# Hybrid diffusion trunk on one core: stores of q, k, v from GpSimd and ScalarE, shared rope tables, residual loaded during the attention, differential softmax normalised on the output

## Chip, cores, metric

The kernel runs on one core of a Trainium2 chip. The metric is device time in microseconds (us), lower is better. Engines are called PE (TensorE), PEld (its weight loads), DVE (VectorE), ACT (ScalarE), POOL (GpSimd) and SP (SyncE); a "q" behind a name is that engine's instruction queue. L12 is line 12 of the kernel file. Layers are counted from 0.

## What is computed

One inference step of a two-layer trunk for 128 context tokens and 1024 latent tokens (a 16 x 64 grid), width 1024, all float32. In each layer:

```python
h = adaln(x, g_attn, m[0], m[1])                  # modulated RMS norm
q, k, v of A, B, C = split(h @ w_in)              # RMS norm on every q and k
q, k of B and C = rope(q, k)                      # latent tokens only
oa = neighborhood_attn(qa, ka, va, cache_na, rpb) # 4 heads of 64, window 8 x 16 with bias
ob = window_attn(qb, kb, vb, cache_sw, sink)      # 8 query heads, 2 key heads, |i-j| <= 128
oc = diff_attn(qc, kc, vc, cache_da, lam)         # 4 heads, all latent keys
x  = x + m[2] * (concat(oa, ob, oc) @ w_out)
x  = x + m[5] * conv_ffn(adaln(x, g_ffn, m[3], m[4]))
```

Each of the attentions also reads 256 cached keys and values; the context tokens attend to each other alone. The six modulation vectors m come from a matrix of 1024 x 6144 per layer. The differential attention is what the change rewrites:

```python
o1 = softmax(q1 @ k1.T) @ v
o2 = softmax(q2 @ k2.T) @ v
o  = rmsnorm(o1 - lam * o2, subln_g) * (1 - lam_init)
```

The outputs are x and, for the context tokens, the keys and values of both layers.

## The kernel before

Activations lie transposed: features on the 128 partitions, the 1156 columns (context, latent, a zero column at each border) along the free axis, cut into three chunks of about 386. A product of float32 matrices is three PE passes over a high and a low part of each operand (`gemm`, L496), so weights and activations are split on ACT and DVE or POOL before use (`wload`, L377 and L378; `norm_apply`, L483 and L484).

The order of the work is written out in `PLAN`: 18 column blocks of the input projection (`inproj`), with the four heads of the differential attention C (`attnC`) among them, "C:14+12" being two blocks interleaved and "c:0" a head. A block of q or k goes through, for each chunk: 24 matmuls, the norm's sum by a ones matrix (L523), the reciprocal root on ACT, DVE and POOL (L441 to L444), its product on POOL (L525), for B and C the rotation with a table loaded from memory (L531 to L536), the split into high and low (L559, L560), and a store to a scratch tensor in memory `d` (L542 to L565). v blocks are transposed on PE and stored likewise (L587), and the context part of k and v goes to the output `kvT` (L528, L580). Each head then reads its q, k and v back from `d` in the layout it needs: q and k by loads issued on POOL (L605 and L615; in C L695 and L699), v by loads on SP.

In `attnC` a pair of score rows (one for each component) of 128 queries and 1280 keys gets its exponentials (L682) and their sums, and then:

```python
735  nc.vector.reciprocal(ss, ss)
736  nc.vector.tensor_tensor(ss, ss, lam, op=ALU.mult)
737  nc.gpsimd.tensor_scalar(P2[0][:, :n], P2[0][:, :n], ss[:, 0:1], 0.0, op0=ALU.mult, op1=ALU.add)
738  nc.vector.scalar_tensor_tensor(P2[0][:, :n], P2[1][:, :n], ss[:, 1:2], P2[0][:, :n], op0=ALU.mult, op1=ALU.add)
```

so that the combined rows are normalised before they are transposed (L649) and multiplied with v (L658). `subln` follows for each pair of heads (L763 to L769), and the pair's output goes to the scratch `odr` (L757).

After the last block come the four heads of A (`attnA`), which normalise on the output instead (`rows_over`, L670: four transposes of the row sums; L905). Its bias tiles are loaded by SP into seven buffers (L855). The residual x (L296, 4.73 MB by the tile's shape) is loaded back behind A in the program's text, from the input in layer 0 and from the scratch `xsp` in layer 1; then B (`attnB`). The output projection has a part for C (i = 1) and one for A (i = 0), both from `odr` (`outproj_part`, L283), and one for B. In layer 0 eight pieces of the modulation matrix (`mod_piece`, four tiles `mraw` of 0.52 MB each, L388; two matmuls a tile, L392) stand four before each of the first two parts, with three buffers.

The program's text doesn't set the order of instructions on the engines: a scheduler with its own model of time fills each engine's queue. Every queue, SP's of transfers among them, then runs strictly in that order.

## Time and profile before

| | us |
|---|---|
| runs shown: median (lowest, highest) of 3 | 3601.14 (3599.38, 3604.77) |
| profiled execution, its own time | 3596.75 |
| its span, first to last instruction | 3595.0 |
| PE busy, share of the span | 3328.8 (93%) |
| DVE | 2146.0 (60%) |
| ACT | 1513.5 (42%) |
| POOL | 1054.7 (29%) |
| mean DMA rate over the span | 91 GB/s |

Busy shares are averages over stages with different limits; the stages, and what ends each wait, tell more. The granted clock (PEclk) is 1 at 2.4 GHz and 0.5 at 1.2 GHz; a mean between them says that a stretch saw both. A wait is put down to the instruction that released it last.

### The profile page before, as it was taken

To read this page: it belongs to the slowest core of one execution; us is meant where nothing else is said; L and a number is where in the kernel's file an instruction comes from. 1 tells how busy PE (TensorE), PEld (TensorE's weight loads), DVE (VectorE), ACT (ScalarE), POOL (GpSimd) and SP (SyncE) were. 2 spreads that over 40 slices of the span, in tenths; PEclk is the share of its full clock that TensorE was granted. 3 is DMA by queue.
4 is the path that set the end of the run, shared out by engine and by line. 5 is a ranking of instruction groups with operands and counts; after the bars stand their busy time and mean duration, and the time that the engine had idled before them with its cause. 6 is when DMAs were issued, how large, how long until landed. Compare 5 with 4: busy or idle time off the path is not lost. (4 is left out here: it accounts for less than half of the span.)

```text
span 3595.0 us, 54059 instructions
## 1 busy us (share of the span) xinstructions
PE 3328.8 (93%) x20334; PEld 3011.7 (84%) x20334; DVE 2146.0 (60%) x4646; ACT 1513.5 (42%) x2909; POOL 1054.7 (29%) x1170
## 2 busy tenths in 40 slices
PE   6799995999999999999997999868999999999999
PEld 4688773767889999999985877746878999999999
DVE  5567783445567755776575767944547544544455
ACT  4456664446432322222243566635674322232222
POOL 6545563011520111111155455532126111111110
PEclk9899997989999999999998999979999999999999
DMA  5543429532112212222134434385201111111112
GB/s 196 141 115 103 115 89 284 159 105 44 56 39 80 86 66 67 88 88 71 47 119 124 125 103 110 93 229 123 56 20 48 39 45 42 42 37 45 43 42 94
DMA packets 190675, 325.02 MB, mean 90 GB/s; under 512 B 58928, under 2 KB 132800, under 8 KB 190032
## 3 DMA queue, kind: packets, MB, share of 16 engines
q1 hardware_dynamic: 176752, 273.67, 24.8%
q0 software_dynamic: 13664, 47.91, 6.4%
q8 instruction: 161, 2.64, 0.3%
q14 instruction: 98, 0.80, 0.1%
HBM read 269.35 MB, written 56.36 MB: 91 GB/s over the span
## 5 line engine op out<-in xcount | busy, mean ns | idle before, releaser
L496 PE MATMUL mm<-h,whl 128*128 128x386 f32 (+2 forms) x4824 | 970.7, 351 | 27.2 <-DVE t L443 21.9
L496 PEld LDWEIGHTS mm<-h,whl 128*128 128x128 f32 x4824 | 881.5, 195 | 56.0 <-DVE t L443 30.9
L496 PE MATMUL s<-h,whl 128*128 128x386 f32 (+2 forms) x3960 | 740.3, 342 | 13.3 <-ACT h L483 6.7
L496 PEld LDWEIGHTS s<-h,whl 128*128 128x128 f32 x3960 | 704.4, 190 | 28.9 <-DVE h L484 13.5
L378 POOL TENSOR_TENSOR whl<-wraw,whl 128x1024 fp32r<-128x1024 f32 x88 | 211.4, 2402 | 1353.3 <-ACT whl L377 1267.2
L682 ACT ACTIVATE P<-P,nm 128x1280 f32<-128x1280 f32 (+4 forms) x360 | 345.5, 961 | 195.7 <-DVE nm L730 85.4
L377 ACT ACTIVATE whl<-wraw 128x1024 fp32r<-128x1024 f32 (+1 forms) x214 | 211.5, 990 | 469.1 <-PE s L496 275.4
L496 PE MATMUL s<-ah,whl 128*128 128x384 f32 (+1 forms) x1268 | 357.0, 342 | 1.6 <-DVE x L914 1.2
L651 ACT ACTIVATE pt<-tb 128x512 f32<-128x512 f32 (+2 forms) x456 | 237.0, 541 | 121.8 <-PE tb L649 119.1
L914 DVE SCALAR_TENSOR_TENSOR x<-mm,m,x 128x128 f32<-128x128 f32 (+3 forms) x357 | 176.1, 514 | 179.1 <-PE mm L496 178.5
L649 PE MATMUL tb<-ident,P 128*128 128x128 f32 x1600 | 264.7, 282 | 14.2 <-DVE P L738 9.5
L914 DVE SCALAR_TENSOR_TENSOR x<-s,m,x 128x128 f32<-128x128 f32 (+3 forms) x347 | 170.0, 513 | 169.9 <-PE s L496 169.5
L658 PE MATMUL pv<-pt,v 128*64 128x128 f32 x3200 | 260.3, 284 | 3.7 <-ACT pt L651 2.9
L649 PEld LDWEIGHTS tb<-ident,P 128*128 128x128 f32 x1600 | 181.8, 141 | 78.8 <-issue 44.4
L496 PE MATMUL mm<-ah,whl 128*128 128x384 f32 (+1 forms) x844 | 244.5, 340 | 1.4 <-DVE x L914 1.4
L496 PEld LDWEIGHTS s<-ah,whl 128*128 128x128 f32 x1268 | 233.8, 189 | 5.9 <-DVE x L914 1.7
L658 PEld LDWEIGHTS pv<-pt,v 128*64 128x64 f32 x3200 | 170.2, 136 | 77.2 <-issue 46.4
L679 PE MATMUL s<-k,q 128*128 128x256 f32 (+2 forms) x816 | 182.7, 339 | 39.9 <-DMA k<-d 28.1
L496 PE MATMUL s<-al,whl 128*128 128x384 f32 (+1 forms) x634 | 215.1, 339 | 0.0
L496 PE MATMUL mm<-o,whl 128*128 128x384 f32 (+1 forms) x792 | 171.8, 352 | 43.4 <-ACT o L636 41.3
L959 ACT ACTIVATE ah<-yv 128x384 fp32r<-128x384 f32 x132 | 69.4, 526 | 277.6 <-DVE yv L957 277.6
L496 PEld LDWEIGHTS mm<-o,whl 128*128 128x128 f32 x792 | 139.7, 192 | 53.6 <-ACT o L636 42.6
(199 smaller groups left out, 5018.7 us busy)
## 6 DMA issues: line engine op xcount, KB each, us to landing
wraw<-wup SPq DMA_DIRECT2D x88, 512.0 KB
mraw<-wmod SPq DMA_DIRECT2D x48, 512.0 KB
mraw<-wmv SPq DMA_DIRECT2D x96, 256.0 KB
wraw<-wdn SPq DMA_DIRECT2D x64, 384.0 KB
k<-d POOLq DMA_DIRECT2D x80, 288.5 KB, 6.0
wraw<-win SPq DMA_DIRECT2D x36, 512.0 KB
rope<-rope SPq DMA_DIRECT2D x36, 386.0 KB
d<-hl SPq DMA_DIRECT2D x28, 386.0 KB
```

The lines of the kernel that those rows point to most:

```text
L377: nc.scalar.activation(hl[:, 0, :n], raw[:, :n], AF.Copy)
L378: lo_eng.tensor_tensor(hl[:, 1, :n], raw[:, :n], hl[:, 0, :n].bitcast(F32), op=ALU.subtract)
L496: nc.tensor.matmul(ps, w_, r_[:, a:b], start=(i == 0), stop=(i == tot - 1))
L649: nc.tensor.transpose(t[:, 128 * j:128 * j + 128], it[0], self.ident)
L651: nc.scalar.activation(pt[:, :n], t[:, :n], AF.Copy)
L658: nc.tensor.matmul(ps[64 * i:64 * i + 64, :128], V[:, vb], pts[g // 4][:, 128 * (g % 4):128 * (g % 4) + 128], start=first[i], stop=left[i] ...
L679: nc.tensor.matmul(dst, q, view(ks[i]), start=(i == 0), stop=(i == 1))
L682: self.nc.scalar.activation(P[:, :n], P[:, :n], AF.Exp, scale=-1.0, bias=nm, accum_out=sums)
L914: nc.vector.scalar_tensor_tensor(xx, ps[:, s - a:e - a], m[:, col + ob, v:v + 1], xx, op0=ALU.mult, op1=ALU.add)
L959: nc.scalar.activation(ah[:, o:o + n], y, AF.Copy)
```

## The change

Seven edits stand together. Stores of q and k (and of the attention outputs of A and C to `odr`) are issued by POOL instead of SP, stores of v by ACT, and the store of k to the output moves behind the split. The rope table of a chunk is kept for the other block of an interleaved pair. The residual is loaded after the last bias load of A's second head, and with it the operands of the output projection for C. The modulation pieces are placed two before the part for C and six before that for A, with five buffers. In C the component rows are combined unnormalised, with the weight lam * sum1 / sum2 for the second, and the output is multiplied by 1 / sum1 for four query blocks at a time; `subln` follows at the second and the last of them.

```diff
-NM0, NMC = 8, 3
+NM0, NMC = 8, 5
@@ run
+                        self.rope = {}
                         gens = [self.inproj(ip, step[0], int(b)) for b in step[2:].split("+")]
...
                 x = xp.tile([128, KT, XW], F32, name="x")
-                for t in range(3):
-                    self.loadx(x, t)
                 ab, abs_ = self.open("oab")
+                with self.tc.issue_after(self.amark[1].ins):
+                    ow1 = self.loado(ab, 1)
+                    for t in range(3):
+                        self.loadx(x, t)
...
-                    for j in todo[4 - 4 * i:8 - 4 * i]:
+                    for j in todo[:2] if i else todo[2:]:
                         self.mod_piece(l, j, ab, self.mm(), NMC)
-                    self.outproj_part(x, ab, i)
+                    self.outproj_part(x, ow1 if i else self.loado(ab, 0), i)
@@ inproj, q and k
-                if not isq and ci == 0:
-                    nc.sync.dma_start(a["kvT"][l, KOUT[b]], qg[:, C0:C0 + SEQ])
                 if g != "A":
-                    cs = ip.tile([128, 2, 386], F32, name="rope", bufs=NR_I)[:, :, :n]
-                    nc.sync.dma_start(cs, a["rope"][0 if g == "B" else 1, :, :, c0:c1])
+                    if (g, ci) not in self.rope:
+                        cs = ip.tile([128, 2, 386], F32, name="rope", bufs=NR_I)[:, :, :n]
+                        nc.sync.dma_start(cs, a["rope"][0 if g == "B" else 1, :, :, c0:c1])
+                        self.rope[g, ci] = cs
+                    cs = self.rope[g, ci]
...
-                            nc.sync.dma_start(dst[:, i, :, c0:c1], hl[:, i, :n].bitcast(F32))
+                            nc.gpsimd.dma_start(dst[:, i, :, c0:c1], hl[:, i, :n].bitcast(F32))
                     else:
-                        nc.sync.dma_start(dst[:, :, c0:c1].rearrange("h p w -> p h w"), hl[:, :, :n].bitcast(F32))
+                        nc.gpsimd.dma_start(dst[:, :, c0:c1].rearrange("h p w -> p h w"), hl[:, :, :n].bitcast(F32))
+                if not isq and ci == 0:
+                    nc.gpsimd.dma_start(a["kvT"][l, KOUT[b]], qg[:, C0:C0 + SEQ])
@@ inproj, v (the store to kvT likewise)
-                nc.sync.dma_start(dst[ci].rearrange("t p c -> p t c"), vs)
+                nc.scalar.dma_start(dst[ci].rearrange("t p c -> p t c"), vs)
@@ attnC
+            sums = ap.tile([128, 8], F32, name="sums", bufs=2)
...
-                    nc.vector.reciprocal(ss, ss)
-                    nc.vector.tensor_tensor(ss, ss, lam, op=ALU.mult)
-                    nc.gpsimd.tensor_scalar(P2[0][:, :n], P2[0][:, :n], ss[:, 0:1], 0.0, op0=ALU.mult, op1=ALU.add)
+                    r = sums[:, q0 + i:q0 + i + 1] if q0 is not None else ss[:, 2:3]
+                    nc.vector.reciprocal(r, ss[:, 0:1])
+                    nc.vector.reciprocal(ss[:, 1:2], ss[:, 1:2])
+                    nc.vector.scalar_tensor_tensor(ss[:, 1:2], ss[:, 1:2], lam[:, 1:2], ss[:, 0:1], op0=ALU.mult, op1=ALU.mult)
                     nc.vector.scalar_tensor_tensor(P2[0][:, :n], P2[1][:, :n], ss[:, 1:2], P2[0][:, :n], op0=ALU.mult, op1=ALU.add)
...
+                if q0 in (2, 6):
+                    R = self.rows_over(sums[:, q0 - 2:q0 + 2], 1)[rows]
+                    oo = O[rows, L0 + 128 * (q0 - 2):L0 + 128 * (q0 + 2)]
+                    nc.vector.tensor_tensor(oo, oo, R, op=ALU.mult)
+                    if h % 2 == 1:
+                        for c0, c1 in NCHUNK[:1] if q0 == 2 else NCHUNK[1:]:
+                            self.subln(ap, O, c0, c1)
             if h % 2 == 1:
-                nc.sync.dma_start(self.odr[OT["C"] + h // 2], O)
+                nc.gpsimd.dma_start(self.odr[OT["C"] + h // 2], O)
@@ attnA
-                nc.sync.dma_start(bt, self.a["bias"][l, h, :, i])
+                self.lastb = nc.sync.dma_start(bt, self.a["bias"][l, h, :, i])
                 bias.append(bt)
+            self.amark[h] = self.lastb
```

The three loads of `oraw` that began `outproj_part` are now the function `loado`, otherwise unchanged. Because of the scheduler the rows of every engine move. Three places matter here.

The first is SP's queue in layer 0, where the last block of the in-projection (d_9) is stored and the loads for A begin (w_4 and d_4 are the v of A's first pair of heads, kc a cache tile). Before, and now:

```order
L531 DMA rope<-rope 128x2x386
L296 DMA x<-xT 128x8x386
L296 DMA x<-xT 128x8x384
L565 DMA d_9_4993<-hl 128x2x386
L296 DMA x<-xT 128x8x386
L374 DMA wraw<-woac 128x1024
L565 DMA d_9_4993<-hl 128x2x384
L757 DMA odr_544<-O 128x1156
L565 DMA d_9_4993<-hl 128x2x386
L618 DMA kc<-kc 128x256
L846 DMA v<-w_4_3744 128x16x64
L847 DMA v<-d_4_3510 128x64
```
```order
L537 DMA rope<-rope 128x2x386
L381 DMA wraw<-woac 128x1024
L628 DMA kc<-kc 128x256
L857 DMA v<-w_4_3788 128x16x64
L858 DMA v<-d_4_3554 128x64
L859 DMA v<-vc 128x128
L866 DMA bias<-bias 128x384 x6
L857 DMA v<-w_4_3788 128x16x64
L858 DMA v<-d_4_3554 128x64
L859 DMA v<-vc 128x128
L866 DMA bias<-bias 128x384
L395 DMA mraw<-wmod 128x1024 x5
```
The residual's three loads and the stores are gone from this place, and the first modulation tiles follow the loads of A's first two heads.

The second is PE in layer 1, at the end of the in-projection (h), where the scores of A (s<-k,q) and the output projection for C (o) begin. Before, and now:

```order
L658 MATMUL pv<-pt,v 64x128 x12
L496 MATMUL mm<-h,whl 128x386 x24
L765 MATMUL tb<-sq,ones_86 128x386
L523 MATMUL mm<-t,ones_86 128x384
L523 MATMUL mm<-t,ones_86 128x386
L496 MATMUL mm<-o,whl 128x386
L496 MATMUL mm<-o,whl 128x384
L679 MATMUL s<-k,q 128x128
L679 MATMUL s<-k,q 128x384
L679 MATMUL s<-k,q 128x256
L496 MATMUL mm<-o,whl 128x386 x5
L496 MATMUL mm<-o,whl 128x384 x5
```
```order
L680 MATMUL tb<-ident,sums 128x128 x4
L668 MATMUL pv<-pt,v 64x128 x4
L503 MATMUL mm<-h,whl 128x386 x24
L776 MATMUL tb<-sq,ones_86 128x384
L530 MATMUL mm<-t,ones_86 128x386
L776 MATMUL tb<-sq,ones_86 128x386
L503 MATMUL mm<-h,whl 128x384 x24
L530 MATMUL mm<-t,ones_86 128x386
L503 MATMUL mm<-h,whl 128x386 x24
L530 MATMUL mm<-t,ones_86 128x384
L530 MATMUL mm<-t,ones_86 128x386
L689 MATMUL s<-k,q 128x128
```
The output projection no longer stands ahead of the first scores; and the last blocks of the in-projection stand without attention work between them.

The third is POOL in layer 0, where the first q block of C (d_12) is finished and head 0 reads it. Before, and now:

```order
L699 DMA k<-d_14_553 64x1154 x4
L704 TENSOR_TENSOR k<-kc,kr 128x256
L534 TENSOR_TENSOR t<-t,rope 128x386
L703 TENSOR_SCALAR kr<-kc,hsel 128x256
L560 TENSOR_TENSOR hl<-qg,hl 128x386
L525 TENSOR_TENSOR qg<-qg,t 128x386
L444 TENSOR_TENSOR t<-t 128x386
L695 DMA q<-d_12_610 32x1156 x8
L534 TENSOR_TENSOR t<-t,rope 128x386
L525 TENSOR_TENSOR qg<-qg,t 128x386
L444 TENSOR_TENSOR t<-t 128x386
```
```order
L709 DMA k<-d_14_553 64x1154 x4
L714 TENSOR_TENSOR k<-kc,kr 128x256
L542 TENSOR_TENSOR t<-t,rope 128x386
L713 TENSOR_SCALAR kr<-kc,hsel 128x256
L532 TENSOR_TENSOR qg<-qg,t 128x386
L568 TENSOR_TENSOR hl<-qg,hl 128x386
L571 DMA d_12_610<-hl 4x32x386
L451 TENSOR_TENSOR t<-t 128x386
L571 DMA d_12_610<-hl 4x32x386
L705 DMA q<-d_12_610 32x1156 x4
L542 TENSOR_TENSOR t<-t,rope 128x386
L705 DMA q<-d_12_610 32x1156 x4
```
The stores to d_12 now stand in this queue, the second of them directly ahead of the load that reads the block.

## Rows read from the trace of the kernel before

**Rows 1.** Stretches: from:to, length, busy time (instructions) by engine, PEclk, DMA share, GB/s.
```profile
440.00:544.00 104.00, 94.87 (x587) 75.62 (x586) 85.97 (x195) 68.44 (x130) 60.67 (x52) 0.95 0.36 104
544.00:571.00 27.00, 0.92 (x2) 0.30 (x2) 6.11 (x11) 3.04 (x6) 13.99 (x23) 0.61 1.13 309
571.00:589.00 18.00, 4.06 (x12) 2.54 (x13) 2.74 (x12) 2.34 (x6) 1.33 (x6) 0.50 1.22 249
...
708.00:737.00 29.00, 17.55 (x63) 6.81 (x62) 4.82 (x11) 4.69 (x10) 8.47 (x33) 0.60 0.93 294
...
2349.00:2384.00 35.00, 2.49 (x5) 1.40 (x5) 6.33 (x13) 3.92 (x8) 15.35 (x30) 0.50 1.15 302
2384.00:2389.00 5.00, 4.62 (x13) 3.50 (x13) 1.62 (x6) 0.00 (x0) 3.62 (x5) 0.50 1.12 277
2491.00:2508.00 17.00, 2.60 (x14) 2.06 (x13) 2.06 (x7) 2.81 (x8) 9.28 (x34) 0.63 0.99 241
2820.00:3540.00 720.00, 720.00 (x4071) 720.00 (x4070) 345.25 (x561) 193.26 (x293) 90.89 (x38) 1.00 0.13 41
```

**Rows 2.** Waits of PE, layer 0, 545 to 620: total us, times, longest.
```profile
PE s L679 <- DMA k<-d: 28.1, 2, 26.2
PE mm L392 <- DMA mraw<-wmod: 11.5, 1, 11.5
```

**Rows 3.** Waits of PE, layer 1, 2345 to 2420, same columns.
```profile
PE mm L496 <- ACT o L636: 30.3, 2, 25.7
```

**Rows 4.** Timeline of SyncE's queue, layer 0: start, length of issue, line, transfer.
```profile
538.12 1.25 SPq L296 DMA_DIRECT2D x<-xT  x2
...
568.00 16.09 SPq L847 DMA_DIRECT2D v<-d  x1
...
585.08 1.38 SPq L388 DMA_DIRECT2D mraw<-wmod  x3
```

**Rows 5.** Chain that ended last, layer 1: start, us, what.
```profile
2352.95 10.37 DMA odr<-O
...
2364.33 17.68 DMA kc<-kc
```

**Rows 6.** Timeline of GpSimd: start, us, instruction, [idle before <- releaser].
```profile
554.51 1.00 POOL L560 TENSOR_TENSOR hl<-qg,hl 128x386 fp32r<-128x386 f32 x1 [1.23 <-ACT hl L559]
...
563.63 2.06 POOL L615 DMA_DIRECT2D k<-d  x4 [7.09 <-DMA d<-hl]
...
1931.58 2.12 POOL L699 DMA_DIRECT2D k<-d  x4 [5.64 <-DMA d<-hl]
...
2363.29 2.05 POOL L615 DMA_DIRECT2D k<-d  x4
...
2498.88 1.03 POOL L605 DMA_DIRECT2D q<-d  x2 [5.96 <-DMA odr<-O]
```

**Rows 7.** DMA issues: transfer, issuer, count, KB each, median us to landing.
```profile
k<-d POOLq DMA_DIRECT2D x80, 288.5 KB, 6.0
```

**Rows 8.** Timeline of PE, columns as in rows 6.
```profile
715.92 1.92 PE L392 MATMUL mm<-mraw,cvz 128*32 128x512 f32 x4 [5.26 <-DMA mraw<-wmod]
...
1935.19 4.48 PE L496 MATMUL mm<-h,whl 128*128 128x384 f32 x24 [1.65 <-DVE t L443]
1951.09 0.44 PE L728 MATMUL s<-k,q 128*128 128x128 f32 x1 [11.42 <-DMA q<-d]
...
2490.56 0.65 PE L670 MATMUL tb<-ident,sums 128*128 128x128 f32 x4
```

**Rows 9.** Groups by line on GpSimd: count, busy us, mean ns, idle before.
```profile
L737 POOL TENSOR_SCALAR P<-P,ss 128x1280 f32<-128x1280 f32 x64 | 91.3, 1426 | 110.4 <-DVE ss L736 62.4 <-ACT hl L559 11.9 <-ACT pt L651 9.6
...
L695 POOL DMA_DIRECT2D q<-d x64 | 32.1, 510 | 13.2 <-PE s L728 6.7 <-DMA d<-hl 6.2 <-issue 0.3
```

**Rows 10.** Line L738 (DVE): its idle time by releaser, who waited for it.
```profile
  POOL P L737: 23.9, 23
...
  PE tb L649: 9.5, 9
```

More of the change, by code (lines that the diff above doesn't have):

```diff
@@ L193, in run @@
                 ap, aps = self.open("A", "right")
+                self.amark = {}
                 for h in range(4):
@@ L275, in run, with loado @@
             xs.close()
-    def outproj_part(self, x, pool, i):
-        nc, a, l = self.nc, self.a, self.l
+    def loado(self, pool, i):
         ow = {}
@@ L282, in outproj_part @@
             raw = pool.tile([128, 2, 388], F32, name="oraw", bufs=2)
-            nc.sync.dma_start(raw[:, :, :c1 - c0], self.odr[2 * i:2 * i + 2, :, c0:c1].rearrange("k p w -> p k w"))
+            self.nc.sync.dma_start(raw[:, :, :c1 - c0], self.odr[2 * i:2 * i + 2, :, c0:c1].rearrange("k p w -> p k w"))
             ow[t] = self.finO(pool, t, {k: raw[:, k, :c1 - c0] for k in range(2)}, 12)
+        return ow
+    def outproj_part(self, x, ow, i):
+        nc, a, l = self.nc, self.a, self.l
         for ob in range(KT):
@@ L541, in inproj @@
                         nc.gpsimd.tensor_tensor(hl[:, 1, 0:SEQ], qg[:, C0:C0 + SEQ], hl[:, 0, 0:SEQ].bitcast(F32), op=ALU.subtract)
-                        nc.sync.dma_start(dst[:, :, 0:SEQ].rearrange("h p w -> p h w"), hl[:, :, 0:SEQ].bitcast(F32))
+                        nc.gpsimd.dma_start(dst[:, :, 0:SEQ].rearrange("h p w -> p h w"), hl[:, :, 0:SEQ].bitcast(F32))
                     s = max(c0, L0)
@@ L556, in inproj @@
                         dd = dst[hh, :, SEQ:].rearrange("p (c r i) -> p c (r i)", c=4, i=16)[:, :, 16 * r0:16 * (r0 + nr)]
-                        nc.sync.dma_start(dd, hl[:, hh, o:o + 64 * nr].rearrange("p (c x) -> p c x", c=4).bitcast(F32))
+                        nc.gpsimd.dma_start(dd, hl[:, hh, o:o + 64 * nr].rearrange("p (c x) -> p c x", c=4).bitcast(F32))
                 else:
@@ L579, in inproj @@
                 if ci == 0:
-                    nc.sync.dma_start(a["kvT"][l, VOUT[b]], vt[:, C0:C0 + SEQ])
+                    nc.scalar.dma_start(a["kvT"][l, VOUT[b]], vt[:, C0:C0 + SEQ])
                 toks = {0: [8, 0, 1], 1: [2, 3, 4], 2: [5, 6, 7]}[ci]
@@ L718, in attnC @@
                     nm = ap.tile([128, 6], F32, name="nm", bufs=4)
-                    ss = ap.tile([128, 2], F32, name="ss", bufs=4)
+                    ss = ap.tile([128, 3], F32, name="ss", bufs=4)
                     qo = C0 if q0 is None else L0 + 128 * (q0 + i)
@@ L734, in attnC @@
                         self.softrow(P2[c], n, prev[c], ss[:, c:c + 1])
[L735 to L737 removed]
+                    r = sums[:, q0 + i:q0 + i + 1] if q0 is not None else ss[:, 2:3]
+                    nc.vector.reciprocal(r, ss[:, 0:1])
+                    nc.vector.reciprocal(ss[:, 1:2], ss[:, 1:2])
+                    nc.vector.scalar_tensor_tensor(ss[:, 1:2], ss[:, 1:2], lam[:, 1:2], ss[:, 0:1], op0=ALU.mult, op1=ALU.mult)
                     nc.vector.scalar_tensor_tensor(P2[0][:, :n], P2[1][:, :n], ss[:, 1:2], P2[0][:, :n], op0=ALU.mult, op1=ALU.add)
+                    if q0 is None:
+                        nc.vector.tensor_scalar(P2[0][:, :n], P2[0][:, :n], r, None, op0=ALU.mult)
                     Pq.append(P2[0])
@@ L745, in attnC @@
                          [(O[rows, qo + 128 * i:qo + 128 * i + 128], 64 * i, 64 * i + 64, lambda z: z) for i in range(2)])
-                if h % 2 == 1:
-                    if q0 < 6:
-                        done = L0 + 128 * q0 + 256
-                        for c0, c1 in NCHUNK:
-                            if c1 <= done and c1 > done - 256:
-                                self.subln(ap, O, c0, c1)
-                    else:
-                        for c0, c1 in NCHUNK:
-                            if c1 > done:
-                                self.subln(ap, O, c0, c1)
+                if q0 in (2, 6):
[5 more added lines that the diff above has]
+                            self.subln(ap, O, c0, c1)
             if h % 2 == 1:
-                nc.sync.dma_start(self.odr[OT["C"] + h // 2], O)
+                nc.gpsimd.dma_start(self.odr[OT["C"] + h // 2], O)
     def subln(self, ap, O, c0, c1):
@@ L906, in attnA @@
             if h % 2 == 1:
-                nc.sync.dma_start(self.odr[OT["A"] + h // 2], O)
+                nc.gpsimd.dma_start(self.odr[OT["A"] + h // 2], O)
     def addx(self, x, ob, ps, a, b, col):
```

## The prediction, made before the changed kernel had run

> **What bounds the kernel now.** I read the stretches first: busy time of each engine, granted clock and DMA share, stage by stage [rows 1]. TensorE (PE) bounds most of the program: in the feed-forward stretch of layer 1, 2820 to 3540, it is busy all 720 us, and nothing in this change touches that. The reader is to see the holes: PE is busy 0.92 of 27 us and 4.06 of 18 us where the attention of group A begins in layer 0 (544 to 589), 2.49 of 35 us at the same place of layer 1 (2349 to 2384), and 17.55 of 29 and 2.60 of 17 us where group B takes over from A. In all five the DMA share is 0.9 or more. In 440 to 544, the end of the in-projection, PE still leaves 9.1 of 104 us.
>
> Then the waits of PE: 26.2 us for the first key load and 11.5 us for a modulation weight in layer 0 [rows 2], 25.7 us for the first output-projection operand in layer 1 [rows 3]. What do those loads wait for? In SyncE's queue [rows 4] the three residual loads (4.73 MB by the tile's shape) start from 538.12; the issue of one small v load then takes 16.09 us, so the modulation loads leave only at 585.08. In layer 1 the chain of waits [rows 5] runs through a 10.37 us store of the C heads' output and a 17.68 us load of a 128 KB cache tile, both in the wake of the same residual loads.
>
> **The sum, part by part** (against the profiled execution: span 3595.0, own time 3596.75 us).
>
> 1. *Residual loaded later, layer 0.* The order puts the residual behind the 12th bias load, in the middle of A, and stores no longer stand on SyncE, so the cache, v, bias and five modulation loads stand free of it. What stays is the dependency: the last rotated block is split at 554.51 + 1.00 = 555.5 on GpSimd [rows 6]; its store takes 0.51 to issue [rows 9], two q loads 1.1, four k loads 2.06 [rows 6], and a k load lands 6.0 us after issue [rows 7]. Between store and k load GpSimd waited 7.09 us in layer 0 and nothing in layer 1 (2363.29) [rows 6]; I take 3, since the residual no longer shares the engines. First scores: 555.5 + 0.5 + 1.1 + 3 + 2.1 + 6.0 = 568, and they run on, with the modulation weights there. Before, steady work began at 589, with 4.06 us done at a granted clock of 0.50 [rows 1], worth 2. Gain 589 - 568 - 2 = 19. Bounds: 5 (the 16.09 us block belongs to the two v loads in small pieces, not the residual) and 25 (no wait for the store).
>
> 2. *The same in layer 1.* The k issue ends at 2363.29 + 2.05 [rows 6]; plus 0.5 for the store and 6.0: 2372 against 2389. The work before 2389, 2.49 + 4.62 us at clock 0.50 [rows 1], is worth 3.5. The new PE order has scores first and the output projection one head later, so the 25.7 us operand is no longer in the way. Gain 13.5; bounds 5 and 20.
>
> 3. *The residual inside A.* 4.73 MB at the 309 GB/s of [rows 1] is 15.3 us of transfers per layer, and most of head 2's bias loads stand behind it. It leaves when head 0 is nearly done and has head 1 to hide behind. I take a loss of 5 over both layers; bounds 0 and 30.6.
>
> 4. *Modulation pieces 2 and 6 instead of 4 and 4, five buffers.* By the PE order the A stage has 8 weight tiles instead of 16, the passage to B 17 instead of 9, the rest 7 as before. A tile costs 1.92 us at the low clock [rows 8], half that, about 1, at full clock: A is 8 us shorter, the passage longer by 8 tiles of 0.52 MB at 294 GB/s, 14.3, less two more tiles already in buffers, 3.6. Net loss 2; bounds a gain of 8 and a loss of 7.
>
> 5. *Passage to B, layer 1.* GpSimd now issues the store of A's output and has B's four k loads behind it, 10 us later than now. But its last q loads already wait for that store, until 2498.88 [rows 6], and PE has no steady work before 2508 [rows 1]. Loss 2; bounds 0 and 5.
>
> 6. *Stores of q, k, v on GpSimd and ScalarE.* 136 stores move to GpSimd at 0.51 us [rows 9], 69 us, against 91.3 us of the multiplication L737 that goes [rows 9]: nothing. The 40 on ScalarE (at most 0.5 us each by the same row) lie on an engine that is busy 68.44 of 104 us in 440 to 544 [rows 1]: nothing. What they give is an earlier store: at the start of C GpSimd stands 5.64 us waiting for one to land, and PE 11.42 us for q [rows 6, 8], much the same in both layers. No longer behind rope and weight loads in one queue, they land sooner. I take 3 a layer: gain 6; bounds 0 and 22.
>
> The Trainium skill's page "DMA: Bandwidth & Descriptors", section "Issuing engines are not separate DMA queues", says that DMAs of all issuers run on the same 16 engines, and that a second issuer saves its issue time alone. By that the 6 us would be 0 and the sum below 6 us worse; the 5.64 us wait is a landing time, which the trace alone cannot split between queue and engines.
>
> 7. *Differential softmax.* Off the path of each block go the 1.43 us multiplication and its hand-over; DVE waited 23.9 us for it in all and PE 9.5 us for what DVE then made [rows 10]. Added are 16 groups of four transposes on PE, 0.65 each by the like group of A [rows 8]: 10.4 us, and 16 multiplications on DVE beside them. I count half the 9.5 as won: loss 5; bounds a loss of 10.4 and a gain of 13.5.
>
> 8. *Consequence for the in-projection.* C now ends sooner, and by the PE order the last four chunks of the in-projection stand alone, each waiting for a bank: 1.65 us at a like place [rows 8]. Three more such places a layer, 10 us; but the C work done earlier fills some of the 9.1 idle us of [rows 1]. Loss 6; bounds 0 and 11.
>
> 9. *Rope tables shared:* 12 loads of 386 KB fewer, on no path shown; 0. The longer A and B bodies keep their cover, PE's own work; if that went, 12 x 1.3 us of transfers would show.
>
> Sum: 19 + 13.5 - 5 - 2 - 2 + 6 - 5 - 6 = 18.5, so 3596.75 - 18.5 = 3578. The median of the runs shown is 3601.14, 4.4 above the profiled execution, so the same 18.5 from the median would be 3583; I keep 3578.
>
> **Rivals.**
>
> *The residual stalls A instead.* It is needed by the output projection on VectorE and stands ahead of the biases. If its 15.3 us show in full in both layers, item 3 is 30.6: 18.5 + 5 - 30.6 = -7, 3604. For it: DMA share already 0.9 and more wherever these loads meet. Against: head 1 has its data by then.
>
> *GpSimd is held by its own stores: slower.* GpSimd runs in order, and the new order has the first q load of C two rows behind the store that it reads. A k load lands in 6.0 us [rows 7], and four k loads of 0.3 MB ahead in the same queue add 3.8: some 10 us for a store, at six places (two starts of C and one of A in each layer), 59 against 18 waited now (5.64 at one start of C in each layer, 7.09 at one of A). That costs 41, and item 6's gain goes: 18.5 - 6 - 41 = -28.5, 3625. It decides if a store on this queue takes over 7 us to land. Against: layer 1's k loads waited for none at 2363.29 [rows 6].
>
> The Trainium skill's "SBUF — State Buffer", section "SBUF: two separate sides", gives a second reason for such a loss: GpSimd cannot write descriptors while VectorE holds the shared port in certain modes. Issue times of 0.51 us beside a busy VectorE [rows 9] show none of that.
>
> *The holes close further.* Upper bounds of items 1, 2 and 6 (25, 20 and 16 taken) with the losses as above: 61 - 20 = 41, 3556.
>
> That the change doesn't do what it says is not to be feared here: the order shows the residual moved and the stores gone from SyncE.
>
> **How the numbers follow.** About 0.2%, 7 us, can be told from no change. Forecast 3578: 0.60, nearly all of it faster (0.57), its own range 3560 to 3592. Residual stall 3604: 0.16, mostly within 0.2% (0.09), else faster (0.05) or slower (0.02). Stores hold GpSimd, 3625: 0.15, slower by 0.14. Holes close further, 3556: 0.09, faster. Together faster 0.71, same 0.13 (0.04 of it from the edges of the forecast and the slower case), slower 0.16. Range 3553 to 3605: it leaves out most of the slower case.
>
> **What would show it.** Right: PE's hole at the start of A is about 22 us in layer 0 and 24 in layer 1, with no wait for modulation weights behind it; no issue of 16 us on SyncE there; the residual's loads lie under a busy PE. Item 7 right: PE has 64 more transposes of sums, and DVE no wait for GpSimd in C. Wrong: waits of PE or DVE for bias or residual after head 1; GpSimd waits for d<-hl of 7 us and more; PE's waits for a bank in the in-projection adding up to over 20 us.

## The result, and the profile after

The changed kernel is slower: median 3642.15 us of 4 runs (3635.49 to 3644.80) against 3601.91 us (3599.38 to 3604.77), a ratio of 1.0109 with a 95% interval of 1.0091 to 1.0126. The prediction, 3578 and faster, was wrong in its sign and by 64 us. The profiled execution took 3635.49 us, its span is 3633.6.

Where the 39 us between the two spans lie is read by cutting each program at four events a layer that every version has: the first norm matmul (sum by ones) of the in-projection, the first scores of C, the last norm matmul, the last product of probabilities with v. P is from the first norm to the first scores of C, I the rest of the in-projection with C, A the attentions A and B with their passage and the parts of the output projection beside them; the digit is the layer. What is left, the feed-forward halves above all, differs by 5 us at most. The first row has lengths in us, the others what each version's profiled execution takes more:

```
                           P0     I0     A0     P1     I1     A1   
before                   84.1  393.9  370.4   85.1  397.8  326.8
after                    +5.5   +7.8  +13.1   +6.4   +5.3   +4.0
stores alone             +8.4   +6.0   +6.8   +8.0   +8.0   +7.3
  q, k on GpSimd alone   +8.8   -0.8   -2.5   +6.7   -2.1   +8.8
  outputs on GpSimd al.  -0.1   +0.9   +9.1   -1.0   +3.7   +7.0
  outputs on ScalarE al. +3.2   +1.5   +4.2   +0.7   +7.5   -2.1
  all, high on SyncE     +1.6   +6.8  +13.2   +1.0  +18.0   -5.3
softmax alone            +1.5   -4.0   -1.3   +1.2   +1.5  -15.6
residual alone           +0.2   +0.0  -13.3   -0.7   +1.1   +5.3
modulation alone         +5.0   -0.3   +1.6   +3.0   -5.3   +1.6
rope alone               +1.1   +0.3   +4.3   +0.3   -0.4   +1.1
softmax, residual        +0.5   -2.7  -11.3   +0.5   -2.0   +8.1
  the same + modulation  +3.8   -5.3  +10.1   -0.0   -3.2   +8.1
after, stores undone     +0.1   -2.5   +6.6   -2.0   -1.4   +8.5
after, modulation undone +6.0   +8.0  -21.9   +5.9   +7.2   +3.3
softmax, residual 0      +6.5   -4.8  -10.5   +2.5   -2.5  -18.2
```

Single executions, each version with an order of its own, differ by 5 to 7 us where an edit should not act (modulation alone in layer 1; P0 of "softmax, residual 0"), and the profiled execution of "outputs on ScalarE" was 8 us above the median of its runs. So an entry below 8 is read only where several versions agree, as in P1, which is 5.9 to 8.0 longer in every version that stores both parts of q and k from GpSimd, and at most 3.2 longer in any other. Both in-projections (P and I together) lose 12 to 13 us, and attention 0 loses 13 instead of gaining. The stretches of the changed kernel at the places of [rows 1] (columns as there):

```profile
557.00:587.00 30.00, 0.23 (x1) 0.00 (x0) 5.01 (x11) 2.05 (x4) 14.34 (x24) 0.50 1.10 271
...
592.00:640.00 48.00, 47.11 (x340) 30.84 (x341) 21.99 (x82) 31.34 (x78) 12.44 (x20) 0.95 1.03 292
640.00:715.00 75.00, 70.82 (x513) 58.30 (x516) 37.71 (x111) 37.74 (x90) 3.62 (x5) 0.93 0.39 91
715.00:730.00 15.00, 10.71 (x52) 3.20 (x44) 1.03 (x3) 1.74 (x4) 5.68 (x19) 0.77 0.95 299
730.00:745.00 15.00, 8.20 (x22) 2.54 (x24) 0.17 (x1) 0.60 (x1) 0.00 (x0) 0.50 1.21 241
745.00:760.00 15.00, 7.92 (x23) 2.07 (x20) 0.00 (x0) 2.43 (x5) 5.45 (x20) 0.50 1.11 340
...
2384.00:2406.40 22.40, 0.00 (x0) 0.00 (x0) 5.07 (x11) 2.05 (x4) 14.27 (x25) 0.53 1.03 246
...
2521.00:2541.00 20.00, 0.85 (x9) 0.44 (x6) 0.69 (x1) 1.26 (x4) 8.26 (x36) 0.61 0.93 195
```

The starts of A are now single holes of 30 and 22.4 us, where before 44 and 40 us passed until steady work (from 544.9, the end of the last norm matmul, to 589, and from 2349 to 2389). New is the passage to B in layer 0: for 45 us PE is busy 27, mostly at a granted clock of 0.50, the lower of its two levels, while the DMA share is 0.95 to 1.21. Just ahead of it, in 640 to 715, the share is only 0.39. The waits of PE over the whole program (total us, times, longest):

```profile
PE s L689 <- DMA k<-d: 55.2, 5, 30.0
PE mm L399 <- DMA mraw<-wmod: 31.4, 9, 15.1
PE s L739 <- DVE nm L741: 26.2, 57, 2.1
PE mm L503 <- ACT o L646: 23.0, 3, 19.1
```

The 11.5 us wait for a modulation weight at the start of A [rows 2] is gone; six small ones, 15.9 us in all, now stand in the passage (the 15.1 is at the program's start). The 25.7 us for the output projection's operand at the start of A in layer 1 [rows 3] is gone too; the 19.1 now stands at the passage to B of layer 1, where before 10.95 was waited for the same thing.

### The profile page after: what moved, and what is told of

Same layout as the page of the kernel before. It is cut to its first block, busy times and chain, and to the rows that moved or that the text cites. A ratio compares the mean times of both kernels' runs of the same rounds, so it can differ in the third digit from the quotient of the medians.

```text
span 3633.6 us, 54021 instructions
## 1 busy us (share of the span) xinstructions
PE 3354.1 (92%) x20398; PEld 3023.7 (83%) x20398; DVE 2140.5 (59%) x4742; ACT 1513.0 (42%) x2909; POOL 1040.4 (29%) x1234
## 5 line engine op out<-in xcount | busy, mean ns | idle before, releaser
L689 PEld LDWEIGHTS s<-k,q 128*128 128x128 f32 x816 | 130.7, 201 | 89.8 <-issue 68.9
L739 PE MATMUL s<-k,q 128*128 128x512 f32 (+2 forms) x400 | 155.2, 425 | 41.6 <-DVE nm L741 26.2
## 6 DMA issues: line engine op xcount, KB each, us to landing
mraw<-wmod SPq DMA_DIRECT2D x48, 512.0 KB, 10.3
```

What stands on the lines that cost most here:

```text
L689: nc.tensor.matmul(dst, q, view(ks[i]), start=(i == 0), stop=(i == 1))
L739: nc.tensor.matmul(s, Q[c][:, qo:qo + 128], K[c][:, ko:ko + w], start=True, stop=True)
```

## The experiments

Each ratio is against runs of the kernel before on the same chip (medians 3600.9 to 3602.7). Every edit is shown from the kernel it starts from.

### One part alone

The kernel before, with one part of the diff. The first has all moved stores (`nc.sync.dma_start` to `nc.gpsimd.dma_start` or `nc.scalar.dma_start`, as in the diff):

> The kernel before, with part (a) alone: stores of q, k, v and of both attention outputs issued by GpSimd and ScalarE, the k store to kvT behind the split. Theory P (the new time sits in GpSimd's queue: a store there holds the loads and the arithmetic behind it): the in-projection with C is 8 to 12 us longer in each layer, the whole 15 to 30 us slower than before. Theory S (it is the softmax): the in-projection stays within 3 us, and the whole gains 5 to 20 us because the small loads at the start of A no longer stand behind stores.

3638.32 us, ratio 1.0105 (1.009 to 1.012): the stores alone cost 37 us, nearly what the whole change costs. P and I take 14 to 16 us a layer and the attentions 14 on top; theory P has less of both (8 to 12 a layer, 15 to 30 in all), and theory S falls.

The second has the part of the diff under `attnC`:

> The kernel before, with the differential softmax normalised on the output alone. Theory S: 10 to 25 us slower, 5 to 12 in each in-projection, of it 10 as PE's 64 extra transposes and the rest as chunks of the in-projection that have no attention work beside them. Theory P: within 6 us of before (the transposes against the multiplication that goes).

3581.75, ratio 0.9948 (0.9931 to 0.9965). 20 us faster, which neither theory had. Nothing is lost in the in-projection, against theory S and my own term, and attention 1 takes 15.6 us less.

The third and fourth:

```diff
-                for t in range(3):
-                    self.loadx(x, t)
                 ab, abs_ = self.open("oab")
+                with self.tc.issue_after(self.amark[1].ins):
+                    ow1 = self.loado(ab, 1)
+                    for t in range(3):
+                        self.loadx(x, t)
```

> The kernel before, with the residual and the operands of the output projection for C loaded behind the 12th bias load, alone. Both theories: the start of A gains, 10 to 30 us over both layers. If the residual's transfers only move their cost into A (rival R), A and the passage to B lose 5 to 13 us a layer and the whole is within 10 us of before; if not, 15 to 30 us faster.

3593.41, ratio 0.9975 (0.9965 to 0.9984): 8 us faster, 13.3 won in attention 0 and 5.3 lost in attention 1: the total is within rival R's 10 us, the gain of attention 0 is not.

```diff
-NM0, NMC = 8, 3
+NM0, NMC = 8, 5
...
-                    for j in todo[4 - 4 * i:8 - 4 * i]:
+                    for j in todo[:2] if i else todo[2:]:
```

> The kernel before, with two modulation pieces before the output projection's part for C and six before that for A, and five buffers, alone; only layer 0 can change. My working: A 8 us shorter, the passage to B 10 longer, so within 5 us of before. Rival: the passage is bound by the transfers of its 17 weight tiles, and the whole is 8 to 15 us slower.

3592.90, ratio 0.9982 (0.9971 to 0.9994): no loss, and the rival falls. Three parts help alone and the fourth takes all of it, so it seemed that undoing the stores must give some 3565.

### Undoing the stores, and splitting them

The changed kernel with the stores back on SyncE:

> The changed kernel with every store back on SyncE; the other parts as changed. If the parts add, as they did alone (softmax -20, residual -8, modulation -9 us against before): 3560 to 3570 us. If the gains overlap (two parts close the same hole): 3575 to 3585. If the loss of the stores needs the other parts or the parts hurt each other, 3590 or more.

3608.72, ratio 1.0019 (1.0009 to 1.0029). The stores give back 33 us when undone, but the rest is still slower than before: the parts do not add. In the table, P and I are as short as they should be; the attentions are not.

Then the stores piece by piece, on the kernel before:

```diff
-                            nc.sync.dma_start(dst[:, i, :, c0:c1], hl[:, i, :n].bitcast(F32))
+                            nc.gpsimd.dma_start(dst[:, i, :, c0:c1], hl[:, i, :n].bitcast(F32))
```

(and the other stores of q and k likewise; in the second run `nc.scalar`)

> The kernel before, with the 128 stores of q and k alone issued by GpSimd (v and the attention outputs stay on SyncE). Theory P (GpSimd is held by issuing them, and the blocks behind come later): 25 to 40 us slower, most of the 37 us that all stores cost. Rival V (the stores of v on ScalarE, or of the outputs on GpSimd, do it): within 8 us of before.

> The same 128 stores issued by ScalarE in place of GpSimd. Theory P: GpSimd has its time back, so at most 10 us slower than before, or faster. Rival Q (it is not the engine but the order: every store off SyncE moves behind arithmetic and the loads come later): 25 us slower or more, as on GpSimd.

3614.47, ratio 1.0034 (1.0021 to 1.0047), and 3606.34, 1.0014 (1.0004 to 1.0025). On GpSimd 13 us, between theory P and rival V, and in the table mostly in P; on ScalarE 5 us, as theory P has it, while rival Q falls. So GpSimd's queue costs, but only half of what theory P put down to these stores. What ScalarE does is seen in its queue: a store of a low part waits 4 us for GpSimd's split, and the next chunk's arithmetic with it.

```diff
-                nc.sync.dma_start(self.odr[OT["C"] + h // 2], O)
+                nc.gpsimd.dma_start(self.odr[OT["C"] + h // 2], O)
...
-                nc.sync.dma_start(self.odr[OT["A"] + h // 2], O)
+                nc.gpsimd.dma_start(self.odr[OT["A"] + h // 2], O)
```

(with the stores of v on ScalarE; then without)

> The kernel before, with the 40 stores of v issued by ScalarE and the 8 of the attention outputs by GpSimd, those of q and k on SyncE. Theory P: within 8 us of before, a gain if the small loads at the start of A no longer stand behind the outputs' stores. Rival V: 20 to 35 us slower.

> The kernel before, with the 8 stores of the attention outputs alone issued by GpSimd. Theory O (the store stands ahead of the k and q loads of the next heads in GpSimd's queue, so their transfers run beside the reading back of the output, and PE waits 19 us instead of 11 for it at the passage to B in layer 1): 8 to 16 us slower, all of it at the passages and starts of the attentions. Rival V (the stores of v on ScalarE cost it): within 4 us of before.

3617.13, ratio 1.0043 (1.003 to 1.0056), and 3618.11, 1.0042 (1.003 to 1.0055): the first lies between its two forecasts, and the second says why: the stores of v cost nothing, eight stores of the outputs cost 15 us, as theory O has it. Rows of GpSimd and of SyncE's queue in the second, at the passage to B of layer 1, and PE's wait there:

```profile
2505.39 0.55 POOL L913 DMA_DIRECT2D odr<-O  x1 [38.11 <-DVE O L911]
2506.05 2.08 POOL L620 DMA_DIRECT2D k<-d  x4
...
2508.76 1.18 SPq L284 DMA_DIRECT2D oraw<-odr  x2
...
PE mm L501 <- ACT o L641: 21.0, 2, 18.9
```

The four k loads of B, 289 KB each, stand behind the store, so they leave with it, and the reading back of the output (`oraw`, from which ScalarE's L641 makes the operand o that PE waits for), issued 2.7 us later, runs beside them. To test this the same stores went to ScalarE, where no load stands behind them:

> The 8 stores of the attention outputs alone moved, as before, but to ScalarE in place of GpSimd (where they alone cost 15 us). Theory O (it is the k and q loads of the next heads behind the store in the same queue, which then share the engines with the reading back): those loads stand free again and start before, PE's wait at the passage of layer 1 is back to about 11 us, and the whole is within 5 us of before. Rival: away from SyncE they come late in any queue: 10 us slower or more.

3602.78, ratio 1.0001 (0.9992 to 1.0011). Theory O holds:

```profile
PE mm L501 <- ACT o L641: 10.5, 1, 10.5
...
2496.78 2.12 POOL L620 DMA_DIRECT2D k<-d  x4 [43.57 <-PE tb L654]
...
2507.91 0.33 ACTq L913 DMA_DIRECT2D odr<-O  x1
```

The k loads go out 11 us ahead of the store again, and PE waits 10.5 us, as before. The passage of layer 0 agrees: PE waits 20.2 us for modulation tiles there with the outputs on GpSimd, 10.3 on ScalarE and 10.4 in the kernel before.

For the stores of C the way is another. At the start of C in the kernel before, rows of ScalarE, GpSimd and SyncE's queue:

```profile
135.42 0.53 ACT L559 ACTIVATE hl<-qg 128x386 fp32r<-128x386 f32 x1 [3.20 <-DVE qg L536]
...
139.68 1.01 POOL L560 TENSOR_TENSOR hl<-qg,hl 128x386 fp32r<-128x386 f32 x1
...
142.95 2.02 POOL L695 DMA_DIRECT2D q<-d  x4 [0.33 <-issue]
146.08 1.95 POOL L695 DMA_DIRECT2D q<-d  x4 [1.10 <-DMA d<-hl]
...
135.97 0.51 SPq L563 DMA_DIRECT2D d<-hl  x1
...
140.71 0.52 SPq L563 DMA_DIRECT2D d<-hl  x1
```

and of ScalarE and GpSimd in the changed kernel:

```profile
136.86 0.53 ACT L567 ACTIVATE hl<-qg 128x386 fp32r<-128x386 f32 x1 [2.67 <-DVE qg L544]
...
142.09 1.00 POOL L568 TENSOR_TENSOR hl<-qg,hl 128x386 fp32r<-128x386 f32 x1
143.04 0.76 POOL L571 DMA_DIRECT2D d<-hl  x1
143.82 1.02 POOL L451 TENSOR_TENSOR t<-t 128x386 f32<-128x386 f32 x1
144.77 0.73 POOL L571 DMA_DIRECT2D d<-hl  x1
148.95 2.03 POOL L705 DMA_DIRECT2D q<-d  x4 [3.44 <-DMA d<-hl]
150.97 0.90 POOL L542 TENSOR_TENSOR t<-t,rope 128x386 f32<-128x386 f32 x1
151.95 2.01 POOL L705 DMA_DIRECT2D q<-d  x4
```

ScalarE has the high part of q ready at 135.95, GpSimd the low part at 140.68. SyncE stored the high part at 135.97, so the four q loads that need it went out at 142.95, before the low part had landed. On GpSimd it is ready at 137.39, but its store stands behind the split that makes the low part, at 143.04; all eight loads come after both, and the last ends at 153.96 instead of 148.03. In the changed kernel the two stores land 5.6 and 6.9 us after their start (at 148.66 and 151.67); in the kernel before GpSimd goes on 5.4 us after the low part's store starts, and in layer 1 12.0 us after it (1935.43 to 1947.41). So a slower landing can be at most 1.5 of the 5.9 us here, and is not what the two layers have in common. From the kernel with all stores moved:

```diff
-                            nc.gpsimd.dma_start(dst[:, i, :, c0:c1], hl[:, i, :n].bitcast(F32))
+                            (nc.gpsimd if i else nc.sync).dma_start(dst[:, i, :, c0:c1], hl[:, i, :n].bitcast(F32))
```

> All stores moved as in the change, nothing else, but the store of the high part of C's q and k back on SyncE (the low part stays on GpSimd). Theory H (the high part is ready early, but in GpSimd's queue its store stands behind the split and other arithmetic; so all eight q loads of the first head come behind both stores): the stretch from the first norm to the first scores of C, 8 us longer in both layers with all stores moved, is within 3 us of before, and the whole is 10 to 20 us faster than with all stores moved, 3618 to 3628. Rival T (GpSimd loses its time to issuing stores, whichever): 3632 or more.

3631.18, ratio 1.0077 (1.0062 to 1.0092). P is longer than before by 1.6 and 1.0 us instead of 8.4 and 8.0, as theory H has it, and the first four q loads went out at 134.53. Counted from the first norm matmul, the low part, which the first scores wait for last, is stored at 73.8 and 69.4 us in the kernel before (layers 0 and 1), at 79.2 and 80.4 with all stores moved, and at 73.5 and 76.1 here. So the high part's stores on GpSimd are what P loses by; but the low part itself comes earlier without them, and the run does not separate this from the earlier loads of the high part. The total fell by 7 us only, outside the 10 to 20 forecast and within a microsecond of theory T, since I1 and A0 of this version are longer (18.0 and 13.2 more than before). Why they are is open.

### The attentions

Which of the remaining parts undoes the gains? The first of these starts from the kernel before and has two parts, the second is the changed kernel with stores and residual undone:

> The kernel before, with the softmax part and the late residual, nothing else. Alone they gave -19 and -9 us. Theory D (the late residual stands ahead of A's bias loads in SyncE's queue, and once the start of A is closed by the softmax part it only costs): 3585 to 3605, PE waiting 15 us and more for the score rows that wait for a bias. Rival M (the modulation pieces and the rope tables are what takes the gains away when all parts but the stores stand together): they add, 3570 to 3578.

> The changed kernel with the stores back on SyncE and the residual back at its old place. Theory D: 3565 to 3585, the best so far. Rival M: 3595 or more.

3586.11, ratio 0.9954 (0.9936 to 0.9972), and 3586.08, 0.9953 (0.9934 to 0.9971). The gains add to less than their sum. In the first PE waits 20 us in all for score rows that a bias load holds up (8.4, 7.9 and 3.8). That is theory D's amount, but for the most part not its cause: the bias loads behind the 8.4 and the 7.9 leave ahead of the residual's (565.01 to 576.34 against 600.06; 2352.36 to 2367.30 against 2380.53), and the softmax part alone has the first of these waits as well, 7.7 us. Only the 3.8 comes behind the residual's loads. A1 loses its gain all the same; the run with the late residual in layer 0 alone shows below how. The second version lies 1 us beyond theory D's range, and neither shows the loss of the four parts together. Shared rope tables alone:

> The kernel before, with the rope tables of interleaved pairs shared, alone. My forecast: within 4 us of before. Rival M: 10 us slower or more, since a table's buffer is held until both blocks have used it.

3599.16, ratio 0.9990 (0.9979 to 1.0): neutral. That left two interactions. The first, with the modulation pieces added to softmax part and late residual:

> The changed kernel with the stores on SyncE and the rope tables unshared: softmax, late residual and modulation pieces. All four together take 23 us more than softmax and late residual alone, 18 of them in the attention of layer 0. If the modulation pieces do it (five weight tiles loaded at once beside the residual and A's first loads): 3600 to 3612, the attention of layer 0 longer than before. If the rope tables do it: 3580 to 3590.

3608.05, ratio 1.0016 (1.0006 to 1.0025): the pieces cost 22 us here, 21 of them in A0, though alone they cost nothing. The same on the changed kernel itself, the pieces four and four with three buffers again:

> The changed kernel with the modulation pieces four and four and three buffers, as before the change; the stores stay where the change put them. Theory M2 (17 of the weight tiles fall into the passage to B, where nothing covers their transfers): the attention of layer 0 is 12 to 22 us shorter than with the change, 3620 to 3630. Rival (with the stores on GpSimd that stretch has another limit): 3636 or more.

3604.46, ratio 1.0015 (1.0005 to 1.0024): 38 us faster than the changed kernel, more than forecast; 35 of it is A0 (348.5 us against 383.5), and nothing else moves by more than 2. PE's order tells why. In the changed kernel, rows of PE and of SyncE's queue, and what the queue waits for there (from 660 to 720):

```profile
617.05 1.05 PE L399 MATMUL mm<-mraw,cvz 128*32 128x512 f32 x4
...
714.33 2.77 PE L399 MATMUL mm<-mraw,cvz 128*32 128x512 f32 x20
720.78 3.75 PE L399 MATMUL mm<-mraw,cvz 128*32 128x512 f32 x8 [2.32 <-DMA mraw<-wmod]
...
688.78 26.50 SPq L381 DMA_DIRECT2D wraw<-wob  x2
715.43 3.09 SPq L395 DMA_DIRECT2D mraw<-wmod  x5
...
SPq L381 <- DVE whl L385: 51.2, 2, 25.8
```

With the pieces undone, PE, SyncE's queue and the stretches; last, PE with the modulation part alone:

```profile
660.12 1.07 PE L399 MATMUL mm<-mraw,cvz 128*32 128x512 f32 x8
...
679.09 1.06 PE L399 MATMUL mm<-mraw,cvz 128*32 128x512 f32 x8
...
661.86 20.94 SPq L395 DMA_DIRECT2D mraw<-wmod  x7
...
640.00:705.00 65.00, 63.90 (x472) 47.61 (x471) 31.00 (x102) 35.23 (x87) 6.87 (x12) 0.97 0.58 169
705.00:720.00 15.00, 14.71 (x82) 11.80 (x80) 8.48 (x16) 0.64 (x2) 4.80 (x30) 1.00 1.13 228
720.00:735.00 15.00, 10.35 (x49) 6.43 (x48) 8.18 (x30) 8.71 (x22) 5.22 (x8) 0.77 0.78 265
```

```profile
680.76 1.92 PE L397 MATMUL mm<-mraw,cvz 128*32 128x512 f32 x14
```

A tile is four of these matmuls. In the changed kernel PE uses the eighth tile at 617.05. Tiles 9 to 13 fill the five buffers by 646.95, and PE comes to the first of them only at 714.33, so the fourteenth leaves at 715.43, after 75 us of A at a DMA share of 0.39. Two weight loads for B's output projection stand ahead of it in SyncE's queue and wait 51.2 us for weight buffers of their own, but there was no buffer for the tile sooner. Then PE has 17 tiles in a row and almost nothing beside them: five from the buffers, twelve as they land, and B's first scores only at 762.14. B's v and cache loads stand among these tiles in SyncE's queue (one v load takes 13 us to issue, at 727.95). The passage, from A's last product with v to B's first scores, takes 44.7 us, where before it was 19.3.

The place in PE's order follows from the program's text: the six pieces stand behind the output projection for C. Two of the runs above, the changed kernel with stores and residual undone and with the stores alone undone, differ only in the late residual (with the operands of that part). With it early the part ends on PE at 677.6, the tiles run from 677.51 amid A's last head, and the passage takes 11.6 us and has none of them; the modulation part alone does the same (680.8, 680.76 and 11.5). With it late it ends at 700.6, the tiles follow at 702.67, behind A's last head as here, and the passage takes 29.4 us. So it takes back what the late residual wins at the start of A (A0 of the two is +5.3 and +6.6). With the pieces undone 16 tiles stand ahead of the part for C; PE uses seven of them from 660.12 to 681.38, amid A's last head, seven more leave from 661.86, and the passage of 19.0 us is filled (PE busy 18.7) by the part for C itself.

In the changed kernel the passage is 15 us longer than with the stores undone. There B's four k loads leave at 692.43, here at 719.69, behind the store of A's output in GpSimd's queue, so that they land among the tiles. The price, then, is not that of the pieces but of what stands ahead of them and beside them. No run changed PE's order and nothing else; this account is read from the traces.

The second interaction, in layer 1, with the late residual in layer 0 only (from the version with softmax part and late residual; the three lines under the last `with` are as they were, one step further in):

```diff
+                if l > 0:
+                    for t in range(3):
+                        self.loadx(x, t)
                 ab, abs_ = self.open("oab")
+                if l == 0:
+                    with self.tc.issue_after(self.amark[1].ins):
...
-                    self.outproj_part(x, ow1 if i else self.loado(ab, 0), i)
+                    self.outproj_part(x, ow1 if i and l == 0 else self.loado(ab, i), i)
```

> The kernel before, with the softmax part, and the late residual in layer 0 alone (layer 1 loads it where the kernel before does). In the runs so far the attention of layer 0 took 11 to 13 us less with a late residual, and that of layer 1 took 16 less with the softmax part and an early residual, but 8 more with a late one. Theory D (in layer 1 the late residual gives back what the softmax part wins): 3567 to 3577, the best so far. Rival N (these are accidents of the scheduled order that do not carry over): 3582 to 3592, as softmax part and late residual in both layers.

3564.50, ratio 0.9891 (0.9872 to 0.9910), beyond the forecast. The stretches from the end of the in-projection in layer 1, first of this version (the last norm matmul ends at 2336.4), then of softmax part and late residual in both layers (2332.0):

```profile
2336.00:2356.00 20.00, 6.41 (x22) 4.83 (x21) 6.43 (x14) 4.86 (x10) 12.73 (x14) 0.57 0.96 329
2356.00:2376.00 20.00, 19.94 (x112) 18.90 (x111) 13.11 (x28) 1.06 (x1) 8.14 (x23) 1.00 1.26 250
2376.00:2396.00 20.00, 19.91 (x154) 15.84 (x153) 14.87 (x54) 14.43 (x36) 5.27 (x10) 1.00 0.96 237
```

```profile
2343.00:2365.00 22.00, 3.55 (x8) 2.00 (x8) 0.36 (x2) 0.70 (x3) 8.56 (x23) 0.50 1.11 203
2365.00:2385.00 20.00, 15.11 (x106) 12.08 (x106) 10.45 (x41) 12.71 (x33) 5.57 (x11) 0.77 0.94 231
2385.00:2405.00 20.00, 15.12 (x100) 11.87 (x101) 6.32 (x25) 9.40 (x25) 3.54 (x5) 0.83 1.11 311
```

The softmax part lets C's last head end before the last blocks of the in-projection, so its output is stored at 2321.95 here (2352.95 in the kernel before [rows 5]) and the output projection for C can run from 2348, while A's k is still being stored and loaded. With the late residual its operands are tied to the same mark, and their loads leave at 2379.58 instead of 2334.91: PE has next to nothing until the scores at 2357.10, and these then wait 7.93 us at 2369.35 for a row that a bias load holds up.

Last, with the shared rope tables added:

> The best so far (softmax part, late residual in layer 0 alone: 3564 us) with the shared rope tables as well. Alone these were within 0.2% of no change. Forecast: 3558 to 3568. If the order that the scheduler makes of it breaks one of the two closed starts of A: 3575 or more.

3562.68, ratio 0.9892 (0.9875 to 0.9909): as forecast, and no different from without. Both versions beat both kernels, by 1.1% and 2.1%.

## Why the prediction was wrong, point by point

*Items 1 and 2, the starts of A: the mechanism was right.* Layer 1: 13.5 forecast; 22.4 us of hole stand against 40, and less the 3.5 of work that was in it that is 14. Layer 0: 19 forecast, 12 measured (30 against 44, less 2). There the last split ends at 569.4, not 555.5, because the in-projection ends 12 us late; and k took 15.7 us from its issue at 571.55 to the scores, not 6.0. The 6.0 is the median of 80 loads, and at this place the kernel before had k loads of 14.2 us already (567.27). Five modulation tiles (2.6 MB) had left at 569.33. With three tiles (modulation undone) the hole is 25.7.

*Item 3, residual inside A: 5 forecast.* In the changed kernel PE waits only 2 us for rows that a bias holds up in layer 0. But the price hangs on the order: with the stores undone such waits add up to 25.6 us over both layers. Of these 15.6 are in the first head, whose bias loads leave ahead of the residual's; 10.0 come behind it. So the rival "the residual stalls A instead" describes a part of that version, and not this one. What the item left out is that the late residual moves the output projection for C, and with it what stands behind (item 4) and what could fill the hole in layer 1 (items 7 and 8).

*Item 4, modulation pieces: this is the first of two steps that failed.* "Net loss 2; bounds a gain of 8 and a loss of 7" is a loss of 38 in the changed kernel, 35 of it in A0. I took the passage as longer by the transfers of eight tiles, less two in buffers, 10.7 us in all, and believed the rest as before. From A's last product with v to B's first scores it is 25.4 us longer (44.7 against 19.3), and A is not 8 us shorter: from its first scores to its last product with v it takes 130.2 us, against 118.5 from steady work on in the kernel before. I had counted the tiles in the passage but not asked what else PE has there. The six pieces stand behind the output projection for C, which the late residual puts at the end of A; so nothing is left in the passage to compute while twelve tiles land one after the other, and B's k loads (item 6) among them, with PE at the lower clock.

*Item 6, stores: the second.* "Gain 6; bounds 0 and 22" is a loss of 33 us by the run that undoes them, 37 alone, some 30 of it in P and I of both layers. I had set the stores' issue time, 69 us, against the 91.3 us of the multiplication that goes, as if GpSimd's mean load mattered. Nor is it 69:

```profile
L571 POOL DMA_DIRECT2D d<-hl x48 | 34.1, 710 | 0.1
...
L573 POOL DMA_DIRECT2D d<-hl x42 | 31.7, 755 | 10.9 <-POOL hl L568 8.9 <-issue 1.7 <-DMA rope<-rope 0.3
```

A store of several strided rows takes 0.71 to 0.77 us to issue, not the 0.51 of a q load [rows 9], 98 us over all 136. What counts is where they stand. The Trainium skill's page "DMA: Bandwidth & Descriptors", section "Issuing engines are not separate DMA queues", had said that another issuer saves its issue time at most; the runs agree that nothing was won. The loss is outside that rule: it is the place of a store among the arithmetic and the loads of its new queue. That is tested for the outputs, and for C's high part in P; for I it is open. The rival "GpSimd is held by its own stores", 3625, had the sign and the queue, but took its 41 us from GpSimd's own waits for a store to land, 59 instead of 18. These waits are 22.1 in the changed kernel (10.6, 7.5 and 4.0) against 26.2 before.

*Item 5, passage in layer 1: 2 forecast, bounds 0 and 5.* The outputs on GpSimd cost 15 us alone, in both passages. I saw that B's k loads stand behind the store, and priced the wait of the q loads, not the reading back that runs beside the k loads.

*Items 7 and 8, softmax and lone chunks: 11 lost forecast, 19 won.* With the stores undone P and I are 6 us shorter, so the 64 transposes don't show in the in-projection; and the earlier output of C, which I had counted only as a loss of cover, is worth 16 us at the start of A in layer 1. With the late residual as well A1 is 8 us longer than before instead, and in the changed kernel 4.

*Item 9, rope: 0 forecast*, within 0.2% measured.

How the 40 us come about, then: against softmax part and late residual (3586), the pieces alone cost 22 us (3608), the stores alone 18 (3604, pieces undone) and both together 56 (the rope tables, neutral, are among them). The two don't add: 16 us appear only when both stand together, and the passage in layer 0 has them. It takes 44.7 us with both, 29.4 with the stores undone, 19.0 with the pieces undone and 18.9 with neither. Undoing the stores gives 33, undoing the pieces 38, and either leaves the kernel at about its old time.

Open: the 6 to 8 us that I loses in both layers when all stores move, but not when q and k or the outputs move alone, which is no more than single executions differ by; the 18 us in I1 of the version with the high part on SyncE; and why A itself is longer in layer 0.

## What to carry to other kernels

Before moving a DMA to another engine's queue, write down for each what it has to stand behind there and what stands behind it: a store that was free to leave when its data was ready waits for arithmetic, and loads that were ahead of it come after. A buffer comes free where the order of the engine that uses it has the use: here five full buffers lay unused for 67 us, and no place in the queue of loads could have changed that. So before work is placed later, look where in that engine's order it will stand, and what else stands there; a stretch of low DMA share just ahead of a wait for a load is the sign. A hole is best closed by work that needs none of the late data, so an edit that moves such work (here the operands of the output projection) is priced by the hole it would have filled. And parts of a scheduled program don't add: three that gave 20, 8 and 9 us alone took 7 together.

## What was not expected of the hardware

Eight stores of 578 KB in another queue cost 15 us (1.0042), and 0 (1.0001) in a third. A passage of 45 us bound by loads ran at a granted clock of 0.50 to 0.77, where the same stretch, with its loads issued earlier, ran at 0.77 to 1.00.
